# Attention values as 128 stationary columns: high and low halves of a key head side by side

## The chip, the cores and the metric

The kernel runs on one core of one Trainium2 chip. The metric is the device time of one execution in microseconds (us); a kernel's time is the median of its runs.

## The reference, cut to what matters

A two-layer decoder trunk on 256 tokens of width 2048: retention and a gated ConvFFN, then sliding-window attention with sinks and ALiBi and a second ConvFFN, all in float32. The change touches the end of the attention:

```python
# 32 query heads, 4 key/value heads, head size 64, blocks of 128 tokens, window 128
scores = einsum('bnqhgd,bnkhd->bnhgqk', q, kb) * (dh ** -0.5)
scores = scores - slopes * dist                      # then masked to the window
probs = softmax(concatenate([scores, sink], -1))[..., :-1]
out = einsum('bnhgqk,bnkhd->bnqhgd', probs, vb)      # the product that is changed
return out.reshape(B, S, Hq * dh) @ w_out
```

## The kernel before, in words

All large products run on TensorE in a rounded 32-bit format. To keep accuracy, every operand is split in two: a high part (a ScalarE cast) and a low part (the original less the high part, a VectorE subtraction). A product then is the sum of three matmuls: high by high, high by low, low by high (`split_products`, L393 to L398). `split_store` (L400 to L406) makes the two parts of an activation.

The weights stream from memory in units of 1 MB. `run_main` (L188) walks through the units in one fixed order and issues the matmuls of one chunk of weights after another (L254 and L256, or L243 to L245). Each unit is loaded by a DMA (L144) and split into hi on ScalarE (L156) and lo on VectorE (L157), up to three units ahead of its use. `split_ahead` decides after each chunk which weight splits are issued next.

Everything that isn't a weight product is a task, a generator that `run_tasks` (L130) resumes between chunks: `yield n` means "go on n steps later". The order in which instructions are issued is the program order of each engine's queue, and nothing reorders it later. So a task's place in the queues of ScalarE and VectorE is set by the step at which it is resumed, behind the weight splits issued at that chunk.

The attention works on pairs of heads: `att_pair` (L686), 16 times. Pairs follow one another every four steps, two for each block of queries, so that three pairs are under way at once at different stages: the scores (L701, TensorE); the maxima (L709 to L716, VectorE); the exponentials (L721, L725, ScalarE); the normalisation (L727 to L732, VectorE); the transposes of the probabilities (L263, TensorE) and their split into pT (L403, ScalarE, and L404, VectorE); the product with the values into the PSUM tile po (L396, TensorE) and two ScalarE copies that stack the two heads into y (L753, L754); one step later the split of y into yT (L403 and L404 again), which the output projection reads. In one step, the tasks are resumed in the order yT of pair n-2, transposes and pT of pair n-1, exponentials of pair n. Queries come from `att_queries` (L679): every second pair has a copy (L368), a join (L369) and a scaling (L378) of qT and two additions of the bias (L660). There are two runs of pairs, ten and six, with a stretch of output projection between them. The PSUM pool `ms` has four buffers, which scores, transposes and po take in turn.

The values are prepared once by `att_values` (L666): v for both token blocks, then one ScalarE cast (L674) and one VectorE subtraction (L675) into vs, with all high parts ahead of all low parts. In the product, lhsT, the stationary operand, is a slice of 64 columns of vs, high or low, and po uses 64 of its 128 partitions for each head of the pair. For each head there are three matmuls over 256 query columns (first token block) and three over 128 (second block): twelve in a group.

Of the kernel before, what the change touches and what calls it, by code (L numbers as in the profile page):

```python
# [9 lines left out]
F32 = mybir.dt.float32  # L10
F32R = mybir.dt.float32r
AF = mybir.ActivationFunctionType
ALU = mybir.AluOpType
# [3 lines left out]
P = 128  # L17
D = 2048
S = 256
NT = S // P  # L20
# [3 lines left out]
KV = 4  # L24
GRP = 8
DH = 64
# [81 lines left out]
class Kernel:  # L108
# [557 lines left out]
    def att_values(self, at, g):  # L666
        v = self.ph.tile([P, NT, 256], F32, tag="qT", name="v", bufs=2)
        for t in range(NT):
            self.nc.vector.scalar_tensor_tensor(
                out=v[:, t], in0=g.ps[:, t, :256], scalar=self.r[:, t : t + 1], in1=self.bv,  # L670
                op0=ALU.mult, op1=ALU.add,
            )
        at["vs"] = x = self.ph.tile([P, 2, NT, 256], F32R, tag="vs", name="vs")
        self.nc.scalar.copy(out=x[:, 0], in_=v)  # L674
        self.nc.vector.tensor_tensor(  # L675
            out=x[:, 1], in0=v, in1=x[:, 0].bitcast(F32), op=ALU.subtract
        )

    def att_queries(self, at, b, g):  # L679
        qT = self.join(g, "qT", 2)  # L680
# [5 lines left out]
    def att_pair(self, at, qT, i, f):  # L686

        nc = self.nc
        kT, vs = at["kT"], at["vs"]
        jj = f // GRP  # L690
        al = self.ph.tile([P, 2, 384], F32, tag="al", name="al", bufs=2)
        nc.sync.dma_start(out=al, in_=self.a["alibi"][f])
        pr = self.ph.tile([P, 2, 384], F32, tag="pr", name="pr", bufs=3)
        soft = self.st.tile([P, 4, NT, 2], F32, tag="soft", name="soft")
        m, nm, es, den = (soft[:, x] for x in range(4))
        pss = [self.ms.tile([P, 512], F32, tag="ms", name="ms") for _ in range(2)]
        where = [slice(0, P), slice(P, P + S)]
        for t in range(NT):
            for s in range(2):
                rows = slice(s * DH, (s + 1) * DH)  # L700
                nc.tensor.matmul(  # L701
                    pss[s][:, where[t]], lhsT=qT[rows, i, t * P : (t + 1) * P],
                    rhs=kT[rows, jj, : (t + 1) * P], start=True, stop=True,
                )
        yield 1
        for s in range(2):
            sink = self.sinks[:, 2 * f + s : 2 * f + s + 1]
            for t in range(NT):
                nc.vector.tensor_tensor_reduce(  # L709
                    out=pr[:, s, where[t]], in0=pss[s][:, where[t]], in1=al[:, s, where[t]],  # L710
                    scale=DH**-0.5, scalar=sink, op0=ALU.add, op1=ALU.max,
                    accum_out=m[:, t, s : s + 1],
                )
        sk = self.sinks[:, 2 * f : 2 * f + 2].unsqueeze(1).broadcast_to([P, NT, 2])
        nc.vector.tensor_scalar_mul(nm, m, -1.0)
        nc.vector.tensor_tensor(out=es, in0=sk, in1=m, op=ALU.subtract)  # L716
        yield 1
        for s in range(2):
            for t in range(NT):
                x = pr[:, s, where[t]]  # L720
                nc.scalar.activation(  # L721
                    out=x, in_=x, func=AF.Exp, bias=nm[:, t, s : s + 1],
                    accum_out=den[:, t, s : s + 1],
                )
        nc.scalar.activation(out=es, in_=es, func=AF.Exp)  # L725
        yield 2
        nc.vector.tensor_tensor(out=den, in0=den, in1=es, op=ALU.add)  # L727
        nc.vector.reciprocal(den, den)
        for s in range(2):
            for t in range(NT):  # L730
                x = pr[:, s, where[t]]
                nc.vector.tensor_scalar_mul(x, x, den[:, t, s : s + 1])  # L732
        yield 2
        pTs = []
        for s in range(2):
            ps = self.ms.tile([P, 512], F32, tag="ms", name="ms")
            self.transposes(ps, [pr[:, s, n * P : (n + 1) * P] for n in range(3)])
            pT = self.ph.tile([P, 2, 384], F32R, tag="pT", name="pT", bufs=2)
            self.split_store(pT.unsqueeze(1), ps[:, :384].unsqueeze(1))
            pTs.append(pT)  # L740
        yield 3
        po = self.ms.tile([P, 2, S], F32, tag="ms", name="po")
        for s in range(2):
            vc = slice((2 * jj + s) * DH, (2 * jj + s + 1) * DH)
            pT = pTs[s]
            self.split_products(
                po[:DH, s], vs[:, :, 0, vc], pT[:, :, :S], start=True, stop=False
            )
            self.split_products(
                po[:DH, s, P:], vs[:, :, 1, vc], pT[:, :, S:], start=False, stop=True  # L750
            )
        y = self.ph.tile([P, S], F32, tag="y", name="y", bufs=2)
        nc.scalar.copy(out=y[:DH], in_=po[:DH, 0])  # L753
        nc.scalar.copy(out=y[DH:], in_=po[:DH, 1])  # L754
        yield 1
        self.attT[f] = x = self.ph.tile([P, 2, S], F32R, tag="yT", name="yT", bufs=12)
        self.split_store(x.unsqueeze(1), y.unsqueeze(1))

# [215 lines left out]
```

## Time and profile before

| | |
|---|---|
| median of 3 runs | 2452.9 us (2451.67 to 2455.12) |
| the profiled execution | 2454.33 us |
| its span, first to last instruction | 2452.5 us |
| TensorE matmuls (PE) | busy 2432.6 us, 99% |
| weight loads (PEld) | busy 2088.7 us, 85% |
| VectorE (DVE) | busy 1600.1 us, 65% |
| ScalarE (ACT) | busy 1230.5 us, 50% |
| chain that ended last | 97% PE |

PE, PEld, DVE, ACT, POOL and SP are TensorE's matmuls, its weight loads, VectorE, ScalarE, GpSimd and SyncE. L396 is line 396 of the kernel. Lines such as L396 and L403 are in helpers, so the tile names (po<-pT,vs) tell which use is meant. In a timeline each row is a start, a length, the engine, line, operation, tiles, shape and a count of instructions merged; in brackets the idle time of the engine before it and what released it. Attention pairs fill the time from about 1520 to 1690 us.

### The profile page before, as it was taken

The numbers are of one execution on the slowest core, as the hardware profiler recorded it, in microseconds if no ns is written. First come the engines' busy times: TensorE is split into PE (matmuls) and PEld (weight loads), VectorE is DVE, ScalarE is ACT, GpSimd is POOL, SyncE is SP. The second block draws the span as 40 slices with busy tenths as digits, with TensorE's granted clock in tenths as the row PEclk, the third lists the DMA queues.
The fourth block names the chain that finished last, engine by engine and source line by source line (L and its number), as shares of the span: only waits on it lengthen the run. The fifth ranks groups of instructions, "written<-read, shape, count | busy, mean of one in ns | idle before, by whom it ended". The sixth has DMA issues, their size and how long they took to land.

```text
span 2452.5 us, 32677 instructions
## 1 busy us (share of the span) xinstructions
PE 2432.6 (99%) x13252; PEld 2088.7 (85%) x13252; DVE 1600.1 (65%) x2198; ACT 1230.5 (50%) x1782; POOL 65.0 (3%) x67
## 2 busy tenths in 40 slices
PE   8999999999999999999999999999999999999998
PEld 6888888888888888888888888888888888888887
DVE  6555655555477775677577765876677477657774
ACT  5444344344445553555355555766555355535553
POOL 3000000000002000000000020000000000000000
PEclk9999999999999999999999999999999999999999
DMA  7455555545455555555555555445455555554553
GB/s 269 175 183 183 191 178 185 192 175 192 172 188 181 197 176 202 189 189 184 195 189 189 181 197 191 166 170 179 173 190 186 203 192 189 181 209 177 191 199 126
DMA packets 68697, 458.28 MB, mean 187 GB/s; under 512 B 8001, under 2 KB 9153, under 8 KB 18241
## 3 DMA queue, kind: packets, MB, share of 16 engines
q1 hardware_dynamic: 68256, 455.13, 52.2%
q8 instruction: 104, 1.70, 0.3%
q10 hardware_dynamic: 288, 1.05, 0.1%
q14 instruction: 49, 0.39, 0.0%
HBM read 454.05 MB, written 2.10 MB: 186 GB/s over the span
## 4 chain that ended last, share of the span: by engine, by line
PE 97%; DMA 1%; POOL 1%; issue 1%; DVE 0%; ACT 0%; POOLq 0%; DVEq 0%; SPq 0%; ACTq 0%
PE mm L254 45%; PE mm L256 22%; PE mm L243 9%; PE mm L245 9%; PE mm L244 9%; PE po L396 1%; PE ms L263 1%; DMA raw<-in_ret_in 1%; PE ms L701 1%; POOL acc L300 1%; PE ms L517 0%; DMA h<-in_xT 0%; DVE lo L157 0%; PE ms L357 0%; ACT hi L156 0%
## 5 line engine op out<-in xcount | busy, mean ns | idle before, releaser
L157 DVE TENSOR_TENSOR lo<-raw,hi 128x1024 fp32r<-128x1024 f32 (+2 forms) x857 | 1020.2, 1208 | 550.8 <-ACT hi L156 550.5
L254 PE MATMUL mm<-xT,hi 128*128 128x512 f32 x3552 | 1121.3, 397 | 5.9 <-DVE xT L314 5.9
L156 ACT CAST hi<-raw 128x1024 fp32r<-128x1024 f32 (+2 forms) x857 | 860.6, 1034 | 530.2 <-PE mm L254 222.1
L256 PEld LDWEIGHTS mm<-xT,lo 128*128 128x128 f32 x3552 | 667.9, 188 | 160.5 <-DVE lo L157 2.9
L256 PE MATMUL mm<-xT,lo 128*128 128x256 f32 x3552 | 699.3, 278 | 1.4 <-DVE lo L157 1.4
L254 PEld LDWEIGHTS mm<-xT,hi 128*128 128x128 f32 x3552 | 543.2, 189 | 11.0 <-ACT hi L156 6.1
L254 PE MATMUL mm<-zT,hi 128*128 128x512 f32 x688 | 216.1, 395 | 0.0
L243 PE MATMUL mm<-hi,xT 128*128 128x512 f32 (+1 forms) x544 | 212.1, 390 | 1.3 <-DVE q L369 1.3
L244 PE MATMUL mm<-lo,xT 128*128 128x512 f32 (+1 forms) x544 | 208.9, 384 | 0.0
L245 PE MATMUL mm<-hi,xT 128*128 128x512 f32 (+1 forms) x544 | 208.9, 384 | 0.0
L615 DVE SCALAR_TENSOR_TENSOR cv<-u,cw,cv 128x255 f32<-128x255 f32 x344 | 158.0, 480 | 6.1
L254 PE MATMUL mm<-yT,hi 128*128 128x512 f32 x512 | 161.3, 396 | 0.0
L256 PEld LDWEIGHTS mm<-zT,lo 128*128 128x128 f32 x688 | 129.2, 188 | 30.5
L368 ACT COPY u<-mm 128x512 f32<-128x512 f32 x86 | 50.4, 586 | 194.5 <-PE mm L256 194.5
L256 PE MATMUL mm<-zT,lo 128*128 128x256 f32 x688 | 135.1, 278 | 0.0
L243 PE MATMUL mm<-hi,zT 128*128 128x512 f32 x344 | 133.8, 389 | 0.0
L244 PE MATMUL mm<-lo,zT 128*128 128x512 f32 x344 | 133.8, 389 | 0.0
L245 PE MATMUL mm<-hi,zT 128*128 128x512 f32 x344 | 133.8, 389 | 0.0
L369 DVE TENSOR_TENSOR u<-mm,u 128x512 f32<-128x512 f32 x86 | 59.4, 691 | 103.6 <-ACT u L368 103.6
L243 PEld LDWEIGHTS mm<-hi,xT 128*128 128x128 f32 x544 | 102.7, 189 | 21.0 <-DVE q L369 1.5
L245 PEld LDWEIGHTS mm<-hi,xT 128*128 128x128 f32 x544 | 102.6, 189 | 20.4
L383 DVE TENSOR_TENSOR h<-mm,h 128x512 f32<-128x512 f32 x112 | 77.4, 691 | 64.8 <-PE mm L256 62.9
(122 smaller groups left out, 1882.7 us busy)
## 6 DMA issues: line engine op xcount, KB each, us to landing
raw<-in_up SPq DMA_DIRECT2D x172, 1024.0 KB, 4.7
raw<-in_ret_in SPq DMA_DIRECT2D x94, 1024.0 KB, 4.7
raw<-in_dn SPq DMA_DIRECT2D x60, 1024.0 KB, 4.8
raw<-in_ret_out SPq DMA_DIRECT2D x32, 1024.0 KB, 4.7
raw<-in_qkv SPq DMA_DIRECT2D x20, 1024.0 KB, 4.7
raw<-in_dn SPq DMA_DIRECT2D x20, 768.0 KB, 4.2
raw<-in_att_out SPq DMA_DIRECT2D x14, 1024.0 KB, 4.8
raw<-in_dn SPq DMA_DIRECT2D x8, 896.0 KB, 4.5
```

What stands on the lines that cost most here:

```text
L156: nc.scalar.copy(out=hi, in_=raw)
L157: nc.vector.tensor_tensor(out=lo, in0=raw, in1=hi.bitcast(F32), op=ALU.subtract)
L243: nc.tensor.matmul(out, lhsT=ah, rhs=hi, start=first, stop=False)
L244: nc.tensor.matmul(out, lhsT=ah, rhs=lo, start=False, stop=False)
L245: nc.tensor.matmul(out, lhsT=al, rhs=hi, start=False, stop=last)
L254: nc.tensor.matmul(out, lhsT=hi[:, sl], rhs=both, start=first, stop=False)
L256: nc.tensor.matmul(out[:, :S], lhsT=lo[:, sl], rhs=act[:, 0], start=False, stop=last)
L263: self.nc.tensor.transpose(out=ps[:, j * P : (j + 1) * P], in_=x, identity=self.ident)
L368: nc.scalar.copy(out=x, in_=g.ps[:, :, S:])
L369: nc.vector.tensor_tensor(out=x, in0=g.ps[:, :, :S], in1=x, op=ALU.add)
L383: self.nc.vector.tensor_tensor(out=h, in0=g.ps[:, :, sl], in1=h, op=ALU.add)
L615: nc.vector.scalar_tensor_tensor(out=c[:, half, d:], in0=u[:, half, : S - d], scalar=w[:, 2 - d : 3 - d], in1=c[:, half, d:], op0=ALU.mult ...
```

## The change

The values are laid out anew: for each token block and each pair of value heads, vs holds four blocks of 64 columns: high of head 0, low of head 0, low of head 1, high of head 1. A slice of two blocks is a stationary operand of 128 columns. Each head has two matmuls over 256 columns and two over 128, with the high and the low probabilities as the moving operand: eight in a group. One half of po's partitions then has the products of the high values, the other those of the low values (the product low by low, left out before, is now in the sum). ScalarE copies the half that lies on the wrong side, and VectorE adds the two halves, after the `yield 1` and ahead of the split of y.

```diff
+        at["vs"] = x = self.ph.tile([P, NT, KV // 2, 4, DH], F32R, tag="vs", name="vs")
+        v = v.rearrange("p t (j s d) -> p t j s d", j=KV // 2, s=2)
+        for s in range(2):
+            self.nc.scalar.copy(out=x[:, :, :, 3 * s], in_=v[:, :, :, s])
+        for s in range(2):
+            self.nc.vector.tensor_tensor(
+                out=x[:, :, :, 1 + s], in0=v[:, :, :, s], in1=x[:, :, :, 3 * s].bitcast(F32),
+                op=ALU.subtract,
+            )
...
         po = self.ms.tile([P, 2, S], F32, tag="ms", name="po")
         for s in range(2):
-            vc = slice((2 * jj + s) * DH, (2 * jj + s + 1) * DH)
-            pT = pTs[s]
-            self.split_products(
-                po[:DH, s], vs[:, :, 0, vc], pT[:, :, :S], start=True, stop=False
-            )
-            self.split_products(
-                po[:DH, s, P:], vs[:, :, 1, vc], pT[:, :, S:], start=False, stop=True
-            )
+            for m, (q, k) in enumerate(((slice(S), slice(S)), (slice(P, S), slice(S, S + P)))):
+                v = vs[:, m, jj, 2 * s : 2 * s + 2].rearrange("p x d -> p (x d)")
+                for x in range(2):
+                    nc.tensor.matmul(
+                        po[:, s, q], lhsT=v, rhs=pTs[s][:, x, k], start=m == 0 and x == 0,
+                        stop=m == 1 and x == 1,
+                    )
         y = self.ph.tile([P, S], F32, tag="y", name="y", bufs=2)
-        nc.scalar.copy(out=y[:DH], in_=po[:DH, 0])
+        nc.scalar.copy(out=y[:DH], in_=po[DH:, 0])
         nc.scalar.copy(out=y[DH:], in_=po[:DH, 1])
         yield 1
+        nc.vector.tensor_tensor(out=y[:DH], in0=po[:DH, 0], in1=y[:DH], op=ALU.add)
+        nc.vector.tensor_tensor(out=y[DH:], in0=po[DH:, 1], in1=y[DH:], op=ALU.add)
         self.attT[f] = x = self.ph.tile([P, 2, S], F32R, tag="yT", name="yT", bufs=12)
         self.split_store(x.unsqueeze(1), y.unsqueeze(1))
```

## Rows read from the trace of the kernel before

**Rows 1.** Busy time by stretch: PE, PEld, DVE, ACT, POOL, clock, DMA share, GB/s.

```profile
1530.00:1581.00 51.00, 51.00 (x345) 43.42 (x344) 43.98 (x134) 37.95 (x104) 0.00 (x0) 1.00 0.49 179
```

**Rows 2.** Timeline, TensorE: one group L396 cut at three ends, loads, transposes, scores.

```profile
1538.29 0.51 PE L396 MATMUL po<-pT,vs 128*64 128x256 f32 x3
...
1538.29 0.68 PE L396 MATMUL po<-pT,vs 128*64 128x256 f32 x6
...
1538.29 1.21 PE L396 MATMUL po<-pT,vs 128*64 128x256 f32 x12
...
1539.28 0.30 PEld L254 LDWEIGHTS mm<-xT,hi 128*128 128x128 f32 x2
...
1549.20 0.81 PE L263 MATMUL ms<-ident,pr 128*128 128x128 f32 x6
...
1552.74 0.93 PE L701 MATMUL ms<-kT,qT 64*128 64x128 f32 x8
```

**Rows 3.** Groups by line and shape, 1500 to 1745: busy us, mean ns, idle before.

```profile
L254 PEld LDWEIGHTS mm<-xT,hi 128*128 128x128 f32 x298 | 45.6, 189 | 3.5 <-issue 3.3
...
L404 DVE TENSOR_TENSOR pT<-ms,pT 128x384 fp32r<-128x384 f32 x32 | 16.2, 549 | 1.7 <-ACT pT L403 1.7
```

**Rows 4.** Instructions of the tile vs: durations min/median/max ns, first and last start.

```profile
L675 DVE TENSOR_TENSOR vs<-v,vs x1: 692/692/692, 1507.2 to 1507.2; 128x512 fp32r<-128x512 f32 x1
```

**Rows 5.** Timeline of ACT, 1544 to 1554.

```profile
1544.17 0.57 ACT L368 COPY qT<-mm 128x512 f32<-128x512 f32 x1
...
1549.66 0.40 ACT L403 CAST yT<-y 128x256 fp32r<-128x256 f32 x1
1549.97 0.85 ACT L403 CAST pT<-ms 128x384 fp32r<-128x384 f32 x2
1550.71 0.41 ACT L721 ACTIVATE pr<-pr,soft 128x128 f32<-128x128 f32 x1
...
1552.58 1.03 ACT L156 CAST hi<-raw 128x1024 fp32r<-128x1024 f32 x1
```

**Rows 6.** Timeline of DVE, 1542 to 1554.

```profile
1542.53 0.42 DVE L404 TENSOR_TENSOR yT<-y,yT 128x256 fp32r<-128x256 f32 x1
...
1546.11 1.22 DVE L157 TENSOR_TENSOR lo<-raw,hi 128x1024 fp32r<-128x1024 f32 x1
...
1548.57 0.34 DVE L709 CUSTOM_DVE_ANT_0 pr<-ms,al,sinks 128x128 f32<-128x128 f32 x1
...
1550.19 1.22 DVE L157 TENSOR_TENSOR lo<-raw,hi 128x1024 fp32r<-128x1024 f32 x1
1551.33 0.42 DVE L404 TENSOR_TENSOR yT<-y,yT 128x256 fp32r<-128x256 f32 x1
1551.66 1.01 DVE L404 TENSOR_TENSOR pT<-ms,pT 128x384 fp32r<-128x384 f32 x2
1553.64 1.23 DVE L157 TENSOR_TENSOR lo<-raw,hi 128x1024 fp32r<-128x1024 f32 x1 [0.96 <-ACT hi L156]
```

**Rows 7.** Timeline of DVE: yT of pair 7, then of pairs 10 and 13.

```profile
1601.84 0.42 DVE L404 TENSOR_TENSOR yT<-y,yT 128x256 fp32r<-128x256 f32 x1
...
1648.51 0.42 DVE L404 TENSOR_TENSOR yT<-y,yT 128x256 fp32r<-128x256 f32 x1
...
1672.37 0.16 DVE L716 TENSOR_TENSOR soft<-sinks,soft 128x4 f32<-128x4 f32 x1
1672.45 0.42 DVE L404 TENSOR_TENSOR yT<-y,yT 128x256 fp32r<-128x256 f32 x1
```

**Rows 8.** Timeline of PE early in the span: a long wait of a matmul.

```profile
44.43 0.65 PE L342 MATMUL ms<-ones,acc 128*128 128x2 f32 x4 [2.83 <-POOL acc L300]
```

**Rows 9.** Busy time by stretch, as in rows 1, right after that wait.

```profile
44.80:48.40 3.60, 3.60 (x11) 2.89 (x11) 1.77 (x4) 0.00 (x0) 0.71 (x1) 0.53 0.41 173
```

More of the change, by code (lines that the diff above doesn't have):

```diff
@@ L672, in att_values @@
             )
[L673 to L676, printed above, removed]
-        )
+        at["vs"] = x = self.ph.tile([P, NT, KV // 2, 4, DH], F32R, tag="vs", name="vs")
[7 more added lines that the diff above has]
+            )
     def att_queries(self, at, b, g):
@@ L743, in att_pair @@
         for s in range(2):
-            vc = slice((2 * jj + s) * DH, (2 * jj + s + 1) * DH)
-            pT = pTs[s]
-            self.split_products(
-                po[:DH, s], vs[:, :, 0, vc], pT[:, :, :S], start=True, stop=False
-            )
-            self.split_products(
-                po[:DH, s, P:], vs[:, :, 1, vc], pT[:, :, S:], start=False, stop=True
-            )
+            for m, (q, k) in enumerate(((slice(S), slice(S)), (slice(P, S), slice(S, S + P)))):
[5 more added lines that the diff above has]
+                    )
         y = self.ph.tile([P, S], F32, tag="y", name="y", bufs=2)
-        nc.scalar.copy(out=y[:DH], in_=po[:DH, 0])
+        nc.scalar.copy(out=y[:DH], in_=po[DH:, 0])
         nc.scalar.copy(out=y[DH:], in_=po[:DH, 1])
         yield 1
+        nc.vector.tensor_tensor(out=y[:DH], in0=po[:DH, 0], in1=y[:DH], op=ALU.add)
+        nc.vector.tensor_tensor(out=y[DH:], in0=po[DH:, 1], in1=y[DH:], op=ALU.add)
         self.attT[f] = x = self.ph.tile([P, 2, S], F32R, tag="yT", name="yT", bufs=12)
```

## The prediction

> **What bounds the kernel now.** I read the windows view first, for a stretch of the attention: TensorE (PE) is busy in all 51.00 of 51 us, VectorE (DVE) in 43.98, ScalarE (ACT) in 37.95 [rows 1]. The page's chain of waits says the same of the whole span. So today time is lost or won on PE. The reader should also see that DVE has only 14% left there, and ask what orders its work and ACT's. For that I read the timelines of PE, ACT and DVE beside each other over one pair of heads, about 8.4 us long; their rows stand with the steps below.
>
> **PE: twelve matmuls become eight.** The timeline cuts today's group L396 at three, six and twelve instructions: three of 256 columns end after 0.51, six after 0.68, twelve after 1.21 us [rows 2]. Less the length of the last one (0.28 or 0.22), the starts are (0.51-0.28)/2 = 0.115 apart for 256 moving columns, and ((0.68-0.22)-3x0.115)/2 = 0.058 for 128. A group takes 6x0.115+6x0.058 = 1.04 us. Its weights have 64 columns. With 128 weight columns the load shows: the two loads that follow the group are together 0.30 long, one is 0.189 [rows 2, 3], so they start 0.11 apart, more than the 0.058 that a 128-column matmul would cover; today the group pays this once, at its end, 0.05. New: 4x0.115 for the 256-column products and 4x0.11 for the 128-column ones, 0.90 against 1.09, a gain of 0.19 per pair, 3 us over 16 pairs. Ends: nothing (the loads hide less than I think) and (1.04-4x0.115-4x0.058)x16 = 5.6 us (they never show). I take the row of the load itself.
>
> The Trainium skill, "TensorE: Matmul & The Clock Gate", section "Back-to-back issue gap", gives about 81 ns for a 128-column matmul with its load in a sustained stream; by that the gain would be some 0.3 us per pair, an estimate of 5 us. The row of the load is of this kernel, so it decides.
>
> **The preparation of vs.** Two copies and two subtractions of half the size replace one and one. The old subtraction took 0.69 us at 1507.2 [rows 4], the first product reads it at 1538.29 [rows 2]. The 31 us between hide it; uncovered, two more small operations would cost under 1 us, once.
>
> **Two DVE adds per pair.** ACT's two copies keep their shape. DVE gets two adds of 64x256, one operand in PSUM. No row has that form. Nearest: the yT subtraction, 128x256, 0.42 us, with a 0.33 spacing to its successor [rows 6]. Two adds then take 0.34+0.42 = 0.76 us. Ends: 0.42 for both, as if the second were free, and 1.02, from the PSUM subtraction on 384 columns, 0.549 with 0.47 to its successor [rows 3]. As busy time alone, 0.67 us more in a pair's 8.4 would still fit into DVE's gap. The order is what matters.
>
> **The wait that the adds put in.** Today ACT makes the yT cast (L403) as soon as it has finished the weight cast: at 1549.66, while DVE works on a weight subtraction (L157, from 1550.19) and reaches its own yT operation at 1551.33 [rows 5, 6]. In the new code y is finished by DVE, and the adds stand in DVE's queue where the yT subtraction stands now, behind that L157. So ACT's yT cast, at the head of an in-order queue, waits until 1551.33+0.76 = 1552.1, that is 2.4 us longer than now. Behind it on ACT stand the two pT casts, the exponentials of the next pair, the qT copy in every second pair, and the weight cast hi; DVE then waits for that hi (it already idles 0.96 for it at 1553.64 [rows 6]), and behind DVE's lo stand the normalisation and the maxima, for which PE waits with its transposes. Today's transposes start at 1549.20, only 0.63 after the normalisation's end at 1548.57 [rows 2, 6].
>
> This closes a ring through ACT and DVE, once per pair. Start to start, from rows 5 and 6: adds to yT cast 0.03 (as from hi, 1552.58+1.03, to lo at 1553.64), yT cast 0.31, pT casts 0.74, exponentials 1.87 (1550.71 to 1552.58), hi to lo 1.06, lo and normalisation 2.46 (1546.11 to 1548.57), maxima 1.62 (to 1550.19), the second lo 1.14, adds 0.76: **9.99 us**. With the qT copy, join and scaling between exponentials and lo it is 1546.11-1544.17 = 1.94 instead of 1.06: 10.87. Today the ring lacks the second lo, adds, yT and pT casts: 1.87+1.06+2.46+1.62 = 7.0 (7.9), below the pace at which pairs come, 59.31/7 = 8.47 (yT subtractions from 1542.53 to 1601.84 [rows 6, 7]), and so hidden. The new ring is not: it, not PE, sets the pace.
>
> **The sum.** The pairs come in two runs, ten and six. First run, seven rings with a successor's exponentials, three of them with qT: 3x10.87+4x9.99 = 72.6 against 59.3: +13.3. Second run, from 1648.51 to 1672.45 [rows 7], 23.9 us for three rings; the later ones have no second lo (at 1672.37 and 1672.45 the yT subtraction follows L716 directly): 10.87+2x8.85 = 28.6: +4.7. From each run PE first uses up its 0.63 of slack: -1.3. The last two pairs of each run have no exponentials behind them but still pass the adds and a cast, about 1.2 each; I count half, +2.4. PE's own 3 us is worth nothing while PE waits, and I leave it out. Sum: +19 us. PSUM: po is held until the adds end, at 1552.1 in today's times, while the next pair's scores start at 1552.74 [rows 2]; no term. The weight splits run several units ahead of PE, so hi and lo being 2 us late cost PE nothing of themselves.
>
> The profiled execution took 2454.33 us, 1.8 outside its span of 2452.5; it lies 1.4 above the median of 2452.9. With +19 it would be 2473.3, the median **2472**.
>
> **Rivals.** (a) Not slower: the ring stays below PE's new pace. Its place is DVE's queue ahead of the adds; it decides below 8.47-0.19 = 8.3 us per ring, so my 9.99 would have to be 1.7 too long, say because the second lo is done before ACT needs y. For it: DVE idles 0.96 per plain pair. Against: that idle time is itself a wait for ACT, in the ring. Then PE's 3 us stay: 2450; with the loads hidden, 2447. (b) Half of the ring's excess is swallowed by slack that I don't see, such as operations overlapping more closely than their starts today show: +9, 2462. (c) The clock: PE waited 2.83 us at 44.43 [rows 8], and in the stretch after it the granted clock was 0.53, in the main the lower of its two levels, 1.2 of 2.4 GHz [rows 9]. PE would now wait 1 to 2 us, some ten times. If each wait brought such a stretch of 3.6 us at half speed, 1.7 us lost, it would be +17 more: 2489. Against: the waits stay shorter than that one. (d) That the change doesn't do what it says: PE keeps 1.09 per pair; this alters nothing while the ring rules.
>
> The same page, "What's actually happening", says that the throttled clock is the default and activity lifts it; that is the rule behind (c).
>
> **How the numbers follow.** Forecast 0.77, (a) 0.11, (b) 0.06, (c) 0.06. The forecast's own range: adds at 0.42 instead of 0.76 take 10x0.34 = 3.4 off, tails at nothing 2.4: +13; adds at 1.02 (10x0.26) and full tails: +24, thus 2466 to 2477. To hold 8 in 10, it reaches down to (b) and a little up towards (c): 2462 to 2480. A change of 0.2%, 4.9 us, is about what a measurement of this kernel can tell from none. Slower by more: forecast, (b) and (c), less a little for (b): 0.87. (a) lies at -3, within: 0.09 and, for hidden loads, 0.04 faster.
>
> **What would show it.** In the changed profile PE waits before L263 on DVE (L732 or L709), 1 us and more per pair; ACT's yT cast shows idle time released by the new DVE adds; the yT subtractions are about 10 and 10.9 us apart; PE's PV group has eight matmuls with 128-column loads at 0.11. Wrong would be: PE without idle time between 1530 and 1690, or DVE's adds done before ACT's weight cast ends.

## The result, and the profile after

The changed kernel took 2475.02 us (median of 5 runs, 2470.85 to 2476.69) against 2453.84 for the kernel before (5 runs). The ratio is 1.0086, with a 95% interval of 1.0074 to 1.0097: slower by 21 us, where +19 and 2472 were forecast. The profiled execution took 2476.69, its span is 2474.9.

First the groups of instructions of the changed kernel between 1500 and 1760 us; the last column is the idle time of the engine just before them and who ended it.

```profile
L263 PEld LDWEIGHTS ms<-ident,pr 128*128 128x128 f32 x96 | 10.8, 143 | 20.8 <-issue 11.7 <-DVE soft L714 8.1
...
L763 DVE TENSOR_TENSOR y<-po,y 64x256 f32<-64x256 f32 x16 | 6.8, 428 | 0.2
L762 DVE TENSOR_TENSOR y<-po,y 64x256 f32<-64x256 f32 x16 | 6.5, 409 | 0.0
L403 ACT CAST yT<-y 128x256 fp32r<-128x256 f32 x16 | 6.5, 406 | 48.4 <-DVE y L763 48.4
```

Two numbers are to be seen. ACT stood idle 48.4 us ahead of its 16 yT casts, each time for the second add (L763). TensorE's weight loads (PEld) stood idle 20.8 us ahead of those of the transposes. In the kernel before, the same row reads:

```profile
L263 PEld LDWEIGHTS ms<-ident,pr 128*128 128x128 f32 x96 | 11.1, 140 | 1.1
```

So the loads of the transposes wait 19.7 us more. The matmuls themselves (PE) stand idle less, since those ahead are still running while a load already waits (1.08 us at 1550.18, against 1.25 for the load); their waits are, in all, how often and the longest:

```profile
PE ms L263 <- DVE pr L737: 8.6, 9, 1.8
PE ms L263 <- DVE soft L714: 5.7, 9, 0.7
```

Neither number is the loss itself; that is read from the turns further down. What the transposes wait for is in the timeline of TensorE after the change: the normalisation (L737) for the first three transposes, the maxima of the next pair (L714) for the other three. These read nothing of the maxima's result; they take a PSUM buffer from the pool that the maxima read from, so the wait is put down to that buffer.

```profile
1546.62 1.04 PE L752 MATMUL po<-pT,vs 128*128 128x256 f32 x8
...
1550.18 0.61 PE L263 MATMUL ms<-ident,pr 128*128 128x128 f32 x3 [1.08 <-DVE pr L737]
1551.49 0.70 PE L263 MATMUL ms<-ident,pr 128*128 128x128 f32 x3 [0.69 <-DVE soft L714]
```

Before, all six ran at once, at 1549.20 [rows 2]. The chain of waits that ended last was PE alone in this stretch before, and now runs through ACT and DVE. Its pieces, start, length and what:

```profile
1543.67 0.85 ACT pT L403 x2
1544.53 1.75 ACT pr L726 x8
...
1546.37 0.48 ACT qT L368
...
1546.88 0.70 DVE qT L369
...
1548.21 1.22 DVE lo L157
...
1549.95 0.81 DVE pr L737 x3
...
1552.38 1.14 DVE lo L157
1553.51 0.33 DVE y L762
...
1553.85 0.44 DVE y L763
...
1554.32 0.02 ACT yT L403
...
1554.63 0.13 ACT pT L403
...
1555.48 1.76 ACT pr L726 x8
```

This is the ring of the prediction, one whole turn from pT cast (1543.67) to pT cast (1554.63), and no instruction of TensorE is in it. Its length is read from DVE's yT subtractions, pairs 0 to 2, 7, 10 and 13:

```profile
1543.80 0.42 DVE L404 TENSOR_TENSOR yT<-y,yT 128x256 fp32r<-128x256 f32 x1 [0.47 <-ACT yT L403]
...
1554.75 0.43 DVE L404 TENSOR_TENSOR yT<-y,yT 128x256 fp32r<-128x256 f32 x1 [0.47 <-ACT yT L403]
...
1564.85 0.42 DVE L404 TENSOR_TENSOR yT<-y,yT 128x256 fp32r<-128x256 f32 x1 [0.47 <-ACT yT L403]
...
1617.04 0.43 DVE L404 TENSOR_TENSOR yT<-y,yT 128x256 fp32r<-128x256 f32 x1 [0.47 <-ACT yT L403]
...
1666.54 0.43 DVE L404 TENSOR_TENSOR yT<-y,yT 128x256 fp32r<-128x256 f32 x1 [0.47 <-ACT yT L403]
...
1695.41 0.42 DVE L404 TENSOR_TENSOR yT<-y,yT 128x256 fp32r<-128x256 f32 x1 [0.47 <-ACT yT L403]
```

A turn with qT work takes 10.95 us, one without 10.10. Seven turns of the first run take 73.24 against 59.31 before [rows 6, 7], three of the second 28.87 against 23.94: +13.9 and +4.9.

### The profile page after: what moved, and what is told of

The parts are those of the page before. It is cut to its first block, busy times and chain, and to the rows that moved or that the text cites. A ratio compares the mean times of both kernels' runs of the same rounds, so it can differ in the third digit from the quotient of the medians.

```text
span 2474.9 us, 32596 instructions
## 1 busy us (share of the span) xinstructions
PE 2440.5 (99%) x13188; PEld 2089.9 (84%) x13188; DVE 1614.7 (65%) x2231; ACT 1231.1 (50%) x1783; POOL 64.9 (3%) x67
## 3 DMA queue, kind: packets, MB, share of 16 engines
q10 hardware_dynamic: 288, 1.05, 0.1%
## 4 chain that ended last, share of the span: by engine, by line
PE 93%; DVE 3%; ACT 2%; issue 1%; DMA 1%; POOL 1%; POOLq 0%; DVEq 0%; SPq 0%; ACTq 0%
PE mm L254 44%; PE mm L256 22%; PE mm L243 8%; PE mm L245 8%; PE mm L244 8%; DVE lo L157 1%; ACT pr L726 1%; PE ms L263 1%; PE po L396 1%; DMA raw<-in_ret_in 1%; POOL acc L300 1%; DVE pr L714 0%; PE ms L517 0%; ACT hi L156 0%; DVE pr L737 0%
```

## The experiments

The theory under test: ACT's queue is in order, its yT cast waits for DVE's adds, and so a ring through both engines sets the pace. Rival 1: DVE has too much work. Rival 2: the eight matmuls with wide weights, or the clock, cost it.

**The split of y one step later.** Nothing is left out; the yT cast moves behind the next pair's exponentials.

```diff
         nc.vector.tensor_tensor(out=y[:DH], in0=po[:DH, 0], in1=y[:DH], op=ALU.add)
         nc.vector.tensor_tensor(out=y[DH:], in0=po[DH:, 1], in1=y[DH:], op=ALU.add)
+        yield 1
```

> The changed kernel with one more step between the adds and the split of y into yT; same work, same adds, only ACT's yT cast moves behind the exponentials of the next pair. Theory (ring: ACT's in-order queue waits for DVE's adds): the ring is open, PE's eight matmuls count, 2451 us, 23 to 25 below the changed kernel, no wait of PE before the transposes. Rival 1 (DVE's added work as such, 0.85 us per pair, is too much): 2475, as changed. Rival 2 (PE's group with 128-column loads, or the clock, costs it): 2475.

It took 2452.71 us beside 2453.39 for the kernel before on the same chip, ratio 0.9996 (0.9987 to 1.0005). One line, with all work kept, gives the 21 us back, within the interval. Groups of this run:

```profile
L263 PEld LDWEIGHTS ms<-ident,pr 128*128 128x128 f32 x96 | 11.0, 140 | 2.4 <-DVE soft L714 0.6 <-issue 0.6
...
L403 ACT CAST yT<-y 128x256 fp32r<-128x256 f32 x16 | 6.4, 400 | 4.1 <-DVE y L763 4.1
```

ACT's wait fell from 48.4 to 4.1 us and the wait of the transposes' loads from 20.8 to 2.4. Rivals 1 and 2 fall: the adds and the matmuls are all still there. The median lies 1.7 us above the expected 2451, and the wait of the transposes is not quite gone.

**The adds alone.** The kernel before, with its twelve matmuls, gets two operations that cost what the adds cost.

```diff
         nc.scalar.copy(out=y[DH:], in_=po[:DH, 1])
         yield 1
+        nc.vector.tensor_tensor(out=y[:DH], in0=po[:DH, 0], in1=y[:DH], op=ALU.max)
+        nc.vector.tensor_tensor(out=y[DH:], in0=po[:DH, 1], in1=y[DH:], op=ALU.max)
```

> The kernel before, with its twelve matmuls, and two DVE operations of the same form as the adds (a maximum of po and its copy y, which leaves y as it was) in the same place ahead of the split. Theory: ring closed without any change on PE, 2474 us (2471 to 2478). Rival 1 (DVE's work): also about 2475. Rival 2 (PE's group or its loads): 2454, as before.

2474.24 us, ratio 1.0086 (1.0070 to 1.0101), the same as the whole change. TensorE's part of the change isn't needed for the loss, and its gain does not show either while the ring sets the pace. Busy time by stretch and a group of this run:

```profile
1520.00:1712.00 192.00, 177.35 (x1068) 142.80 (x1067) 144.47 (x397) 114.72 (x291) 0.00 (x0) 1.00 0.41 147
```

```profile
L263 PEld LDWEIGHTS ms<-ident,pr 128*128 128x128 f32 x96 | 10.6, 140 | 21.4 <-issue 11.3 <-DVE soft L709 9.0
```

The loads of the transposes wait as in the changed kernel, and the granted clock is 1.00 (2.4 GHz) through all the attention, so the loss needs no slower clock.

**The products alone.** The changed kernel less the two adds; the sum of the two halves is left out.

```diff
-        nc.vector.tensor_tensor(out=y[:DH], in0=po[:DH, 0], in1=y[:DH], op=ALU.add)
-        nc.vector.tensor_tensor(out=y[DH:], in0=po[DH:, 1], in1=y[DH:], op=ALU.add)
```

> The changed kernel without the two adds (the sum of the two halves is left out): eight matmuls, wide loads, new layout of vs. Theory: only PE's gain is left, 0.19 us a pair, 2451 us (2449 to 2453). Rival 1: 2451 too. Rival 2: 2470 or more.

2450.41 beside 2453.39, ratio 0.9988 (0.9979 to 0.9997): 3.0 us faster, with an interval from 0.7 to 5.2. This is what the change is worth on TensorE.

**Adds that nobody waits for.** The adds stay in their place in DVE's queue and read the same buffers, but write where nobody reads; y is split without them.

```diff
-        nc.vector.tensor_tensor(out=y[:DH], in0=po[:DH, 0], in1=y[:DH], op=ALU.add)
-        nc.vector.tensor_tensor(out=y[DH:], in0=po[DH:, 1], in1=y[DH:], op=ALU.add)
+        z = pr[:, 0, :S]
+        nc.vector.tensor_tensor(out=z[:DH], in0=po[:DH, 0], in1=y[:DH], op=ALU.add)
+        nc.vector.tensor_tensor(out=z[DH:], in0=po[DH:, 1], in1=y[DH:], op=ALU.add)
```

> The changed kernel with the two adds in the same place and of the same form, but their result goes to a tile that nobody reads, and y is split as the copies left it (so the sum of the halves is left out of the output). DVE works as much, po is held as long; ACT doesn't wait. Theory: 2451 to 2454 us, DVE busy as in the changed kernel, ACT's yT cast with no idle time ahead of it. Rival 1 (DVE's work) and a third one (po's PSUM buffer held longer): 2470 to 2475.

2451.77 us, ratio 0.9994 (0.9985 to 1.0003). Groups:

```profile
L763 DVE TENSOR_TENSOR pr<-po,y 64x256 f32<-64x256 f32 x16 | 6.5, 409 | 0.0
...
L403 ACT CAST yT<-y 128x256 fp32r<-128x256 f32 x16 | 6.4, 401 | 0.1
```

DVE does the same work and po is still held until the adds have read it, yet ACT's idle time ahead of the yT cast is 0.1 us in all and the loss is gone. It was the wait, not the work and not the PSUM buffer.

**The adds doubled**, 0.85 us more in the ring: two more lines as the two adds, with ALU.max. This changes the values of y.

```diff
         nc.vector.tensor_tensor(out=y[DH:], in0=po[DH:, 1], in1=y[DH:], op=ALU.add)
+        nc.vector.tensor_tensor(out=y[:DH], in0=po[:DH, 0], in1=y[:DH], op=ALU.max)
+        nc.vector.tensor_tensor(out=y[DH:], in0=po[DH:, 1], in1=y[DH:], op=ALU.max)
```

> The changed kernel with two more DVE operations of the same form (a maximum of po and y, so the numbers change) right behind the adds, 0.85 us more in the ring of every pair. Theory: each of the ten rings with exponentials, and in part the last two pairs of each run, get longer by 0.85: 10 us more than the changed kernel, 2485 us (2482 to 2488). Rival (the wait costs by being there, once per pair, and PE's own pace absorbs what is added): 2475 to 2478.

2486.2 us, ratio 1.0131 (1.0114 to 1.0148). The time follows the length of the ring, as its yT subtractions in DVE's timeline show:

```profile
1543.89 0.42 DVE L404 TENSOR_TENSOR yT<-y,yT 128x256 fp32r<-128x256 f32 x1 [0.47 <-ACT yT L403]
1555.77 0.43 DVE L404 TENSOR_TENSOR yT<-y,yT 128x256 fp32r<-128x256 f32 x1 [0.47 <-ACT yT L403]
1566.79 0.43 DVE L404 TENSOR_TENSOR yT<-y,yT 128x256 fp32r<-128x256 f32 x1 [0.47 <-ACT yT L403]
```

Turns of 11.88 and 11.02 us: each 0.92 or 0.93 longer than in the changed kernel, where 0.85 were expected.

**The adds ahead of the second weight subtraction.** The adds are handed to the next pair's task, which issues them right behind its maxima. A pair whose adds nobody has taken by its own next step issues them itself.

```diff
-        at = {}
+        at = {"sums": []}
...
+        while at["sums"]:
+            at["sums"].pop()()
         yield 1
...
+        def sums():
+            nc.vector.tensor_tensor(out=y[:DH], in0=po[:DH, 0], in1=y[:DH], op=ALU.add)
+            nc.vector.tensor_tensor(out=y[DH:], in0=po[DH:, 1], in1=y[DH:], op=ALU.add)
+        at["sums"].append(sums)
         yield 1
-        nc.vector.tensor_tensor(out=y[:DH], in0=po[:DH, 0], in1=y[:DH], op=ALU.add)
-        nc.vector.tensor_tensor(out=y[DH:], in0=po[DH:, 1], in1=y[DH:], op=ALU.add)
+        if sums in at["sums"]:
+            at["sums"].remove(sums)
+            sums()
```

> The changed kernel with the adds behind the maxima of the next pair and ahead of the second weight subtraction, which so leaves the ring. ACT's yT cast still waits for the adds, but 1.14 us less. Theory: rings of 8.94 and 9.82 us instead of 10.08 and 10.96: 2464 us (2460 to 2467), between both kernels. Rival (a wait of ACT for DVE costs the same whatever stands ahead of it): 2475.

2462.77 us, ratio 1.0039 (1.0024 to 1.0054), between the two kernels as expected. DVE's timeline:

```profile
1543.12 0.42 DVE L404 TENSOR_TENSOR yT<-y,yT 128x256 fp32r<-128x256 f32 x1
...
1552.93 0.42 DVE L404 TENSOR_TENSOR yT<-y,yT 128x256 fp32r<-128x256 f32 x1
...
1561.89 0.42 DVE L404 TENSOR_TENSOR yT<-y,yT 128x256 fp32r<-128x256 f32 x1
```

Turns of 9.81 and 8.96: one weight subtraction of 1.14 is out of the ring.

**The adds at once.** They stand behind the copies, a step earlier.

```diff
-        yield 1
         nc.vector.tensor_tensor(out=y[:DH], in0=po[:DH, 0], in1=y[:DH], op=ALU.add)
         nc.vector.tensor_tensor(out=y[DH:], in0=po[DH:, 1], in1=y[DH:], op=ALU.add)
+        yield 1
```

> The changed kernel with the adds issued at once behind the copies, a step earlier. In DVE's queue they then stand ahead of the maxima of the next pair; ACT's yT cast comes long after them and waits for nothing. Theory: that ring is open, but the maxima, whose PSUM buffer the transposes take, wait for PE's product, ACT's copies and the adds: product to transposes 1.03 + 0.74 + 0.85 + 0.75 + hops = 3.5 us where PE has 2.85 between them, 0.6 us per pair for some 13 pairs, less PE's gain: 2459 us (2456 to 2462). Rival (DVE adds between ACT's copies and the split cost 20 us wherever they stand): 2475.

2454.95 us, ratio 1.0007 (0.9997 to 1.0016). The ring is open, as expected, though ACT's yT casts do wait for the adds in six of 16 pairs, 4.9 us in all. But 4 us less was lost than I said: the transposes waited for the adds only twice, 0.9 us in all, and not 0.6 us in some 13 pairs. The step of the expectation that failed is in DVE's and TensorE's rows:

```profile
1547.70 0.35 DVE L714 CUSTOM_DVE_ANT_0 pr<-ms,al,sinks 128x128 f32<-128x128 f32 x1
...
1547.98 0.48 DVE L714 CUSTOM_DVE_ANT_0 pr<-ms,al,sinks 128x256 f32<-128x256 f32 x1
```

```profile
1547.82 0.52 PE L263 MATMUL ms<-ident,pr 128*128 128x128 f32 x3 [0.42 <-DVE y L762]
```

The fourth transpose starts at 1547.82, before the maxima of the first head are done (1547.98 + 0.48). So here it doesn't wait for the maxima's PSUM buffer but for the one that the adds release. The pool seems to hand out the buffer that is released first in program order, and moving the adds changed which one that is; the second half of this is inferred.

**One step later, but not for the last pair.**

```diff
+        if f < KV * GRP // 2 - 1:
+            yield 1
```

> As e1 (the split of y one step after the adds), but the last of the 16 pairs keeps its split right behind the adds, since the output projection is waiting for it. In e1 PE waited 0.7 us for that yT. Theory: 0.5 to 1 us below e1, 2451.5 us, and 2 to 3 below the kernel before (ratio 0.999). Rival (the remaining 2 us between e1 and the kernel without adds lie in the adds' work on DVE): 2452.7, as e1.

2452.75 beside 2453.95, ratio 0.9998 (0.9989 to 1.0007). Neither a difference from the other late split nor a gain over the kernel before is shown. The edit did only part of what it was for. With the other late split, the output products wait for the last yT twice, 0.27 us for its cast and 0.42 for its subtraction; here the second wait is gone, the first is still there, and a new one of 0.22 (for L443) comes behind it. So the late split repairs the change, and that it makes the change pay is not shown: by the medians about 2 us lie between it and the products alone. In part these may be waits that remain, 2.4 us before the loads of the transposes, where the run with the products alone has 1.4:

```profile
L263 PEld LDWEIGHTS ms<-ident,pr 128*128 128x128 f32 x96 | 11.1, 140 | 1.4
```

The intervals of these runs overlap, so neither the 2 us nor where they lie is settled.

## Why the prediction was right, step by step

The mechanism came out as forecast, and no large errors cancelled in the number: +19 was forecast, +21 measured, and the two terms that missed were both too small.

- **Eight matmuls.** Forecast: 0.90 against 1.09 us per group, 3 us in all. In the changed kernel, the group starts at 1538.40 and the next weight product at 1539.28: 0.88, where it was 1.05 up to the same point (1538.29 to 1539.34), so 0.17 less per pair against a forecast of 0.19. Eight loads span 1.01, one is 0.19, so they start (1.01-0.19)/7 = 0.117 apart on the mean. With 0.115 for each 256-column product, (0.88-4x0.115)/4 = 0.105 is left for each of 128 columns. The products alone gained 3.0 us. Right, and the row of the load was the right guide. The Trainium skill ("TensorE: Matmul & The Clock Gate", section "Back-to-back issue gap") gives about 81 ns for a 128-column matmul with its load in a sustained stream. That is less than the 0.105 us left here, so it does not fit this kernel.

```profile
1538.29 1.01 PEld L752 LDWEIGHTS po<-pT,vs 128*128 128x128 f32 x8
```

```profile
1538.40 1.04 PE L752 MATMUL po<-pT,vs 128*128 128x256 f32 x8
1539.28 0.68 PE L254 MATMUL mm<-xT,hi 128*128 128x512 f32 x2
```

The last row in the kernel before:

```profile
1539.34 0.67 PE L254 MATMUL mm<-xT,hi 128*128 128x512 f32 x2
```

- **Preparation of vs.** Hidden, as said: the products-only run has it too and is faster.
- **The two adds.** Forecast 0.76, measured 0.85: 0.41 and 0.43 long, starting 0.42 apart. I had let the second start after 0.33, as after today's yT subtraction. This is the term that was too small.
- **The wait and the ring.** Forecast 9.99 and 10.87 us per turn, measured 10.10 and 10.95; the difference is about the adds' 0.09. The runs confirm the ring at three places, the wait, the adds and the second weight subtraction; its other links are read from the chain and not cut one by one. With the wait cut, the loss vanishes at the same work; longer by 0.9 or shorter by 1.1 per turn, the time moves by +11 us (1.0131 less 1.0086) and -12 us (1.0039 less 1.0086).
- **The sum.** Seven and three turns: forecast +13.3 and +4.7, measured +13.9 and +4.9. For the slack used up and the last pairs of each run I had -1.3 and +2.4. The slack was read to the start of the maxima, 1548.57; the normalisation itself ended at 1548.66, so the slack read there was 0.54 and not 0.63:

```profile
1547.65 1.01 DVE L732 TENSOR_SCALAR pr<-pr,soft 128x128 f32<-128x128 f32 x4
```

From the first score product to the last matmul of the norm behind the attention, the changed kernel needs 244.5 us (1522.1 to 1766.6), the one before 222.3, the one with the adds alone 243.4. That leaves 22.2-18.8 = 3.4 us for these ends in the changed kernel and 21.1-18.8 = 2.3 with the adds alone, whose turns are as long; 1.1 were forecast. This is the other term that was too small; its two parts were not measured apart.
- **Rivals.** (a) fell: DVE's 0.96 of idle time was in the ring, as its "against" said. (b) fell: nothing was swallowed. (c) came true in part: the clock fell after some of the waits, in three stretches and not ten, and not at the price of 17 us, see below. (d) fell.

## What to carry to other kernels

Before putting an instruction of one engine between two of another, write down the ring it closes: what stands ahead of it in its own queue, what stands behind the waiting one, and back to the start, with start-to-start times, and compare the turn with the pace of the work. Here 0.85 us of work on an engine with time to spare cost 21 us, and one step of delay for the waiting instruction, with nothing else changed, gave all of it back. A gain on the engine that was the bound is worth nothing in the stretch where a ring has taken over.

## What the runs showed of the hardware that I had not expected

The clock fell in the attention though the waits were short. Busy time by stretch of the changed kernel (columns as in rows 1; the third number from the end is the granted clock):

```profile
1550.20:1555.20 5.00, 4.31 (x16) 3.52 (x17) 4.46 (x17) 1.75 (x4) 0.00 (x0) 0.66 0.16 23
1571.20:1576.20 5.00, 4.27 (x16) 3.53 (x17) 4.47 (x17) 1.76 (x4) 0.00 (x0) 0.66 0.13 21
1622.00:1627.00 5.00, 4.43 (x15) 3.54 (x16) 4.45 (x12) 2.23 (x5) 0.00 (x0) 0.66 0.26 87
```

A mean of 0.66 means that about two thirds of each stretch were at the lower level, 1.2 GHz. Before the clock fell, PE had waited 1.08 and 0.69 us in the first stretch, 1.55 and 0.69 in the second, and 1.81 once in the third. With the adds alone it waited 1.36 and 0.69 us one after the other, from about 1568.4, and the clock stayed at 1.00, so the length of the waits alone doesn't tell. I had taken the 2.83 us of [rows 8] as a sign that shorter waits are safe. In the ring it cost nothing that shows: the turns are as long as with the adds alone, where the clock stayed up, since PE isn't what the ring waits for. The third stretch lies behind the first run, where PE sets the pace again. There the next yT subtractions, of pairs 8 and 9, are 9.10 us apart, and 7.69 with the adds alone; that may be part of the 1.1 us by which the ends of the two kernels differ. Of the five runs of the changed kernel, the two with a mean clock of 0.996 took 2476.28 and 2476.69 us, the three with 0.998 2470.85 to 2475.02, which points the same way. No run here separates it.

Two adds over 64 partitions with one operand in PSUM started 0.42 us apart, a whole length of the first, where the yT subtraction lets its successor start after 0.33 of its 0.42 [rows 6]. Two pT subtractions, which read PSUM too, take 1.01 together at 0.55 each [rows 3, 6], so an operand in PSUM alone doesn't make the difference; what does, no run here separates.
